# A two-block fp32 model on one core: first products from unscaled inputs, split weight queues, convolutions by pairs

## The chip, the cores and the metric

One core of a Trainium2 chip runs the whole program. The metric is device microseconds (us) of one execution. Engines are named as in the profile: PE (TensorE; PEld is its weight load), DVE (VectorE), ACT (ScalarE), POOL (GpSimd), SP (SyncE, which issues the transfers).

## The reference

The model has 512 tokens of width 1024, all in fp32: a first block (two gated feed-forward parts, a mixer of sparse attention and a state-space scan, and a gate, "ple"), and a second block of two layers. What matters here is the end of the first and the start of each layer of the second:

```python
def first_block(x, p, ...):
...
        h = h + 0.5 * swiglu(rmsnorm(h, norm_ffn2[i]), ffn2_w1[i], ffn2_w3[i], ffn2_w2[i])
        gate = jax.nn.sigmoid(rmsnorm(h, norm_ple[i]) @ w_ple_gate[i])
        h = h + gate * (p[i] @ w_ple[i])
    return rmsnorm(h, norm_final)
...
def second_block(x, c, ...):
...
    c_act = jax.nn.silu(c)
    for l in range(DEPTH_2):
        mod = c_act @ w_ada[l] + b_ada[l]
        shift, scale, gate = jnp.split(mod, 3, axis=-1)
        h = rms_norm(x, norm_g[l]) * (1.0 + scale[:, None, :]) + shift[:, None, :]
        u = h @ w_in[l]
        rg_x, rg_z, ml_x, ml_o, ml_z = jnp.split(u, split_pts, axis=-1)
        y_rg = rglru(causal_depthwise_conv(rg_x, ...), ...) * jax.nn.silu(rg_z)
        y_ml = mlstm_branch(ml_x, ml_o, ...) * jax.nn.silu(ml_z)
        y = jnp.concatenate([y_rg, y_ml], axis=-1) @ w_out[l]
        x = x + gate[:, None, :] * y
    return rms_norm(x, final_g)
```

## The kernel before, in words

**Layout.** An activation is held transposed, as 8 tiles `h[d]` of 128 channels by 512 tokens. Each fp32 product is made of three matmuls 128x512 (`mm3`, L121): high part of the weight by high part of the input, high by low, low by high. An input tile is split into `xnh` (made on ACT) and `xnl` (on DVE).

**Weights.** All weights come as 304 chunks of 8 blocks of 128x128 (512 KB) in the order of use (`Stream`, L56). SP loads a chunk into `wstage`, ACT makes its high part `whi` (L96), DVE its low part `wlo` (L98). `get` (L108) hands out a block; when it hands out the fifth block of a chunk, it queues both parts of the chunk after the next, one behind the other. Engines run their instructions in the order in which the program queues them, so a part stands in ACT's or DVE's queue at the place where `get` was called. `hold` and `release` keep back this queueing at the end of `ple` and of `out0`.

**Norms.** `Norm` adds the squares of the tiles (ACT squares, DVE and POOL add). `early` sums the first seven tiles over the channels by matmuls with a column of ones, `mean` the last one; `rsqrt` is a chain of small DVE operations and gives `ncol`; `part2` spreads it by four PE transposes to a row `nrow` (ACT copies it out of PSUM).

**The two seams.** At the start of layer 0 (`between`, L1348) and layer 1 (`renorm`, L1378) the norm is formed from the last tile of `ple` or of `out0`. Then `modulate` (L1320) makes the eight input tiles: `mt` = h by the row (DVE and POOL in turn), `xnh` on ACT, `mx` and `xnl` on DVE. The first products of a layer (`proj4`, L1490) are the four output tiles 16 to 19 (`ml_x`), which are accumulated side by side, input tile by input tile. Each is copied into a padded tile `cpad`, and a causal convolution of four taps follows on DVE for all four (`ml_in`: one `conv` with L1507, three with L1509), then the order string `LAYER` (L1385): P24 is the product of output tile 24, U24 its use, qkv0 the block-diagonal products, and so on. Layer 0 also scales x by the norm of block 1 and stores it for the residual (`residual`, L1367, as `aside`).

**Beside ffn2**, `second_prepare` forms the modulation: 48 rows of `w_ada` are loaded and reduced on DVE (`adaj`, L1219). The gate's input `p` is loaded and split there too (`split_p`, L2072).

Of the kernel before, what the change touches and what calls it, by code (L numbers as in the profile page):

```python
# [31 lines left out]
T = 512  # L32
# [3 lines left out]
CH = 8  # L36


R1, R2 = 0.27, 0.26
# [8 lines left out]
GAPS = {"base": 288, "ffn1": 320, "ffn2": 0, "lay": 320, "mix2": 224, "ple": 256}  # L48
# [7 lines left out]
class Stream:  # L56
# [4 lines left out]
    SPLIT = 2  # L61

    def __init__(self, k, dram, nchunks):
        self.k, self.dram, self.n = k, dram, nchunks
        self.order = []
        self.stage, self.hi, self.lo = {}, {}, {}
        self.loaded = self.split_done = 0
        self.pos = 0
        self.hold = False
# [14 lines left out]

    def split(self, upto):
        k = self.k
        while self.split_done < min(upto, self.n):
            c = self.split_done
            self.load(c + 1)
            st = self.stage.pop(c)  # L90
            hi = k.whi.tile([128, CH * 128], F32R, name="whi")
            lo = k.wlo.tile([128, CH * 128], F32R, name="wlo")
            n = 2 if c < 2 else 1
            for i in range(n):
                s = slice(i * CH * 128 // n, (i + 1) * CH * 128 // n)
                k.nc.scalar.activation(hi[:, s], st[:, s], AF.Copy)  # L96
                eng = k.nc.gpsimd if c * i == 1 else k.nc.vector
                eng.tensor_sub(lo[:, s], st[:, s], hi[:, s].bitcast(F32))  # L98
            self.hi[c], self.lo[c] = hi, lo
            self.split_done += 1  # L100
            self.load(c + 1 + self.AHEAD)
# [28 lines left out]
class Norm:  # L130
# [3 lines left out]
    def __init__(self, k, n, pool=None, tail=False):  # L134
        self.k, self.n, self.i = k, n, 0
        self.tail, self.head = tail, None
        self.pool = pool or k.work
        self.acc = []

    def add(self, src, scale=1.0):  # L140
# [4 lines left out]
        if own:  # L145
            sq = self.pool.tile([128, T], F32, name="nacc", bufs=3 if self.pool is k.work else 6)
# [3 lines left out]
        if own:  # L150
            self.acc.append(sq)
        elif i % 2:
            k.nc.gpsimd.tensor_add(self.acc[1], self.acc[1], sq)  # L153
        else:
            k.nc.vector.tensor_add(self.acc[0], self.acc[0], sq)
        self.i += 1
        if self.i == self.n - self.tail:
            eng = k.nc.vector if self.tail else k.nc.gpsimd
            eng.tensor_add(self.acc[0], self.acc[0], self.acc[1])
# [1016 lines left out]
def second_prepare(k, pool, ins):  # L1176
# [15 lines left out]
    for l in range(2):  # L1192
# [8 lines left out]
        L.bif = k.const2.tile([128, 8], F32, name=f"bif{l}")  # L1201
        L.v = lambda name, l=l: k.vec[:, VEC[f"{name}.{l}"][0]:VEC[f"{name}.{l}"][0] + VEC[f"{name}.{l}"][1]]
# [13 lines left out]
        def acc(i, L=L, boxes=boxes):  # L1216
# [3 lines left out]
                                   op0=OP.mult, op1=OP.add, accum_out=L.mod[:, i:i + 1])  # L1220

# [21 lines left out]
        for i in range(24):  # L1243
            step(1.4, acc, i)
            if i < 21:
                step(0.1, load, i + 3)
            if i % 12 == 7:
                step(0.3, fold, i // 12)
                if i < 12:
                    step(0.1, wload, 1)  # L1250

# [24 lines left out]
def ple(k, pool, xs, norm, pt, on_tile, early):  # L1276
# [3 lines left out]
    def gate1(m, pg):  # L1280
        ts[m] = pool.tile([128, T], F32, name="pleg", bufs=2)
# [16 lines left out]
    for m in range(8):  # L1298
# [12 lines left out]
        k.ws.hold = m == 7  # L1311
# [4 lines left out]
    early()  # L1316


def modulate(k, l, norm, gg, scr):
# [4 lines left out]
    with k.tc.tile_pool(name=f"modulate{l}", bufs=3) as tmp:  # L1324
        def scale(d):
            t = tmp.tile([128, T], F32, name="mt", bufs=4)
            if d % 2:
                nc.gpsimd.tensor_mul(t, k.h[d], norm.row)
            else:
                v.tensor_mul(t, k.h[d], norm.wide)  # L1330
            ts.append(t)
        for d in range(3):
            scale(d)
        for d in range(8):
            x = tmp.tile([128, T], F32, name="mx")
            hi, lo = xtile(k, "xnh"), xtile(k, "xnl")
            nc.scalar.activation(hi, ts[d], AF.Identity, scale=gg[:, d:d + 1], bias=L.mod[:, d:d + 1])
            v.tensor_scalar(x, ts[d], gg[:, d:d + 1], L.mod[:, d:d + 1], op0=OP.mult, op1=OP.add)
            if d + 3 < 8:
                scale(d + 3)  # L1340
            v.tensor_sub(lo, x, hi.bitcast(F32))
            xs.append((hi, lo))
            if d == 1:
                k.ws.release()
            k.dbg(f"hh{l}{d}", x)
    return xs


def between(k, scr, nf, ng):

    nc, v = k.nc, k.nc.vector
    gg = k.work.tile([128, 8], F32, name="gg")
    gf = k.vec[:, VEC["norm_final"][0]:VEC["norm_final"][0] + 8]
    v.tensor_mul(gg, gf, k.lay[0].gs)
    nf.part1(root=False)
    ng.mean()
    ms = k.work.tile([128, 4], F32, name="nmt", bufs=2)
    v.scalar_tensor_tensor(ms, nf.ms, 1e-6, ng.ms, op0=OP.mult, op1=OP.add)  # L1360
    ng.col = k.work.tile([128, 4], F32, name="ncol", bufs=2)
    rsqrt(k, ng.col, ms)
    ng.part2()
    xs = modulate(k, 0, ng, gg, scr)
    rsqrt(k, nf.col, nf.ms)

    def root():  # L1367
        nf.part2()

    def residual(d):  # L1370
        v.scalar_tensor_tensor(k.h[d], k.h[d], gf[:, d:d + 1], nf.row, op0=OP.mult, op1=OP.mult)
        nc.sync.dma_start(scr["x"][d], k.h[d])
        k.dbg(f"x2{d}", k.h[d])
    return xs, [root] + [lambda d=d: residual(d) for d in range(8)]


def renorm(k, l, norm, scr):
    norm.part1()  # L1378
    norm.part2()
    xs = modulate(k, l, norm, k.lay[l].gs, scr)  # L1380
    return xs, [lambda d=d: k.nc.sync.dma_start(scr["x"][d], k.h[d]) for d in range(8)]
# [85 lines left out]
def layer(k, l, xs, aside, ins, scr, norm, out):  # L1467
# [4 lines left out]
    with ExitStack() as st:  # L1472
        pool = st.enter_context(k.tc.tile_pool(name=f"lay{l}", bufs=1))
        room(pool, "lay")
# [15 lines left out]
        def proj4(ms):  # L1490
            pp = [bank(k) for _ in ms]
            for d in range(8):
                for ps, m in zip(pp, ms):
                    mm3(k, ps, k.ws.get((win, d, m)), xs[d], d == 0, d == 7)
            return pp
# [30 lines left out]
        G = k.ps.tile([128, T], F32, name="pm", bufs=2)  # L1526
# [698 lines left out]
```

## Time and profile before

| | |
|---|---|
| median of 3 runs (lowest, highest) | 1997.06 us (1995.61, 1997.36) |
| profiled execution: its own time; span | 1996.86 us; 1995.1 us |
| mean granted PE clock | 0.982 |
| PE busy | 1931.2 us (97%) |
| DVE, ACT, POOL busy | 1311.4 (66%), 821.4 (41%), 164.4 us (8%) |

Busy time is the time in which an engine works on an instruction. A granted clock of 1.00 is PE's level of 2.4 GHz, 0.50 its level of 1.2 GHz. In a timeline a start is followed by a duration; matmuls overlap, so the distance of two starts is the time that one takes from the next.

### The profile page before, as it was taken

The page shows a single profiled execution, that of the slowest core. Times are in us where ns is not written, and L with a number is a line of the kernel's source. Part 1 is how long each engine was busy: PE and PEld are TensorE (multiplying, and loading weights), DVE is VectorE, ACT ScalarE, POOL GpSimd, SP SyncE. Part 2 cuts the span into 40 slices and gives each one's busy share as a digit, 9 for nine tenths or more (in the row PEclk, how much of TensorE's full clock was granted, in tenths as well). Part 3 has the DMA queues.
Part 4 walks back from the last instruction along what each step waited for, and adds up shares of the span by engine and source line. Part 5 has one row for each costly group of instructions (what it writes and reads, how often), then busy time and mean ns, then how long its engine had stood idle before and what let it go on. Part 6 is the DMA issues. An engine that isn't in the chain of part 4 may idle for free. (4 is left out here: it accounts for less than half of the span.)

```text
span 1995.1 us, 24709 instructions
## 1 busy us (share of the span) xinstructions
PE 1931.2 (97%) x9320; PEld 1581.3 (79%) x9320; DVE 1311.4 (66%) x2157; ACT 821.4 (41%) x1233; POOL 164.4 (8%) x225
## 2 busy tenths in 40 slices
PE   8999999998999999999999799999999899999997
PEld 6888888887867888888878687888888677887886
DVE  7766576678655575665666675887763666877843
ACT  5323232436555432232244445555432354555521
POOL 1000000111233100000001100101000100101001
PEclk9999999998899999999999899999999899999999
DMA  5335445465301365455433143222242243222241
GB/s 184 103 116 154 158 139 159 143 194 171 103 1 33 117 218 180 158 197 190 162 104 92 55 147 118 74 75 86 88 153 87 64 156 109 70 89 86 74 155 56
DMA packets 101400, 240.10 MB, mean 120 GB/s; under 512 B 24472, under 2 KB 37528, under 8 KB 101280
## 3 DMA queue, kind: packets, MB, share of 16 engines
q1 hardware_dynamic: 100592, 237.82, 37.6%
q8 instruction: 73, 1.20, 0.2%
q10 hardware_dynamic: 688, 0.70, 0.1%
q14 instruction: 47, 0.39, 0.1%
HBM read 216.19 MB, written 21.10 MB: 119 GB/s over the span
## 5 line engine op out<-in xcount | busy, mean ns | idle before, releaser
L98 DVE TENSOR_TENSOR wlo<-wstage,whi 128x1024 fp32r<-128x1024 f32 (+1 forms) x305 | 377.3, 1245 | 147.6 <-ACT whi L96 143.8
L96 ACT ACTIVATE whi<-wstage 128x1024 fp32r<-128x1024 f32 (+1 forms) x306 | 314.0, 1045 | 139.9 <-PE pasecond L126 43.1
L276 ACT ACTIVATE t<-t 128x512 f32<-128x512 f32 x44 | 27.9, 634 | 158.5 <-DVE t L275 158.5
L127 PE MATMUL pahead<-xnh,wlo 128*128 128x512 f32 x208 | 81.3, 391 | 3.4 <-DVE wlo L98 3.4
L125 PE MATMUL pahead<-xnh,whi 128*128 128x512 f32 x208 | 83.3, 400 | 0.0
L153 POOL TENSOR_TENSOR nacc<-nacc,nsq 128x512 f32<-128x512 f32 x20 | 26.8, 1343 | 680.9 <-ACT nsq L149 680.9
L126 PE MATMUL pahead<-xnl,whi 128*128 128x512 f32 x208 | 81.1, 390 | 0.0
L125 PE MATMUL pbfirst<-xnh,whi 128*128 128x512 f32 x176 | 70.4, 400 | 7.6 <-ACT whi L96 6.5
L125 PE MATMUL pbhead<-xnh,whi 128*128 128x512 f32 x192 | 76.9, 400 | 0.0
L1509 DVE SCALAR_TENSOR_TENSOR conv<-cpad,vec,conv 128x512 f32<-128x512 f32 x96 | 72.2, 752 | 5.6
L127 PE MATMUL pbhead<-xnh,wlo 128*128 128x512 f32 x192 | 75.5, 393 | 0.0
L126 PE MATMUL pbhead<-xnl,whi 128*128 128x512 f32 x192 | 75.3, 392 | 0.0
L126 PE MATMUL pbfirst<-xnl,whi 128*128 128x512 f32 x176 | 69.5, 395 | 0.3 <-DVE xnl L222 0.3
L127 PE MATMUL pbfirst<-xnh,wlo 128*128 128x512 f32 x176 | 69.2, 393 | 0.0
L125 PE MATMUL pbsecond<-xnh,whi 128*128 128x512 f32 x176 | 68.9, 392 | 0.0
L125 PE MATMUL pafirst<-xnh,whi 128*128 128x512 f32 x176 | 68.7, 390 | 0.0
L127 PE MATMUL pafirst<-xnh,wlo 128*128 128x512 f32 x176 | 68.6, 390 | 0.0
L127 PE MATMUL pbsecond<-xnh,wlo 128*128 128x512 f32 x176 | 68.5, 389 | 0.0
L126 PE MATMUL pbsecond<-xnl,whi 128*128 128x512 f32 x176 | 68.5, 389 | 0.0
L126 PE MATMUL pafirst<-xnl,whi 128*128 128x512 f32 x176 | 68.5, 389 | 0.0
L127 PE MATMUL pasecond<-xnh,wlo 128*128 128x512 f32 x176 | 68.5, 389 | 0.0
L125 PE MATMUL pasecond<-xnh,whi 128*128 128x512 f32 x176 | 68.5, 389 | 0.0
(762 smaller groups left out, 5229.9 us busy)
## 6 DMA issues: line engine op xcount, KB each, us to landing
wstage<-in_wpack_dram SPq DMA_DIRECT2D x304, 512.0 KB, 3.7
adaw<-in_wada_dram SPq DMA_DIRECT2D x48, 512.0 KB, 4.5
scr_v<-vv SPq DMA_DIRECT2D x16, 256.0 KB, 2.2
vr<-scr_v SPq DMA_DIRECT2D x16, 256.0 KB, 4.4
xr<-scr_x SPq DMA_DIRECT2D x16, 256.0 KB, 5.8
h<-in_xT_dram SPq DMA_DIRECT2D x8, 256.0 KB, 5.8
s5vw<-scr_wq SPq DMA_DIRECT2D x64, 32.0 KB, 2.0
s5vb<-in_s5bq_dram SPq DMA_DIRECT2D x8, 256.0 KB, 2.7
```

The costliest lines, as they stand in the source:

```text
L96: k.nc.scalar.activation(hi[:, s], st[:, s], AF.Copy)
L98: eng.tensor_sub(lo[:, s], st[:, s], hi[:, s].bitcast(F32))
L125: mm(ps, w[0], x[0], start=start, stop=False)
L126: mm(ps, w[0], x[1], start=False, stop=False)
L127: mm(ps, w[1], x[0], start=False, stop=stop)
L153: k.nc.gpsimd.tensor_add(self.acc[1], self.acc[1], sq)
L276: nc.scalar.activation(t1, t1, AF.Silu)
L1509: v.scalar_tensor_tensor(c, xp[:, 1 + j:1 + j + T], w(j), c, op0=OP.mult, op1=OP.add)
```

## The change

1. **First products from raw input.** The four first output tiles of a layer are formed from x = h·g (g the norm's gain times 1 + scale), before the norm is known. These raw tiles are split as soon as each `h[d]` of `ple` or `out0` is ready (`split_raw`). The products run in the order `RAW`: input tiles 0 to 6 of each output tile first, the eighth last. The norm is formed between them (`hooks`: `early`, `mean` and `part2` after products 10, 13 and 17 in layer 0, after 1, 3 and 9 in layer 1). Afterwards each output tile is multiplied by `nrow` on DVE, and a bias `L.sw` is added on ACT (`raw_pad`). `L.sw` is the shift times these weights; it is formed beside ffn2 by 4 more transfers, 4 more DVE reductions and 8 PE transposes per layer.
2. **Input tiles of the other products** are made one operation ahead, spread over the raw products by hooks: `mt` = (h·g)·row on DVE in one operation, `xnh` on ACT, `xnl` on DVE from `mt` and the bias. POOL and `mx` are no longer used.
3. **Weight parts.** The high part is queued when the fourth block of a chunk is handed out (`HI` = 3), the low part at the seventh (`LO` = 6). `hold` and `release` are gone at the seams.
4. **Convolutions** run as two calls of two tiles.
5. **Residual.** h is stored raw in `ple` and scaled in `out0` (8 DVE operations, 4 transposes); the second one is stored in `out0`.
6. **p** is loaded and split at the start of `ple`; squares of tile 6 in `ple` are added after the last tile's gate.

```diff
     SPLIT = 2
+    HI, LO = 3, 6
...
     def get(self, *blocks):
...
-        self.split(c + 1 + (0 if self.hold else self.SPLIT if r >= CH // 2 else self.SPLIT - 1))
+        if not self.hold:
+            self.high(c + self.SPLIT + (r >= self.HI))
+        self.split(c + 1 + (0 if self.hold else self.SPLIT - 1 + (r >= self.LO)))
...
+        step(1.4, sacc, 0)
+        step(0.1, sload, 3)
+        for i in (1, 2, 3):
+            step(1.4, sacc, i)
...
+def split_raw(k, src, g, hi, lo):
+
+    k.nc.scalar.activation(hi, src, AF.Copy, scale=g)
+    k.nc.vector.scalar_tensor_tensor(lo, src, g, hi.bitcast(F32), op0=OP.mult, op1=OP.subtract)
+    return hi, lo
...
+    def scale(d):
+        t = k.ytile("mt")
+        v.scalar_tensor_tensor(t, k.h[d], gg[:, d:d + 1], norm.wide if d == 0 else norm.row, op0=OP.mult, op1=OP.mult)
+        ts.append(t)
+
+    def tile(d):
+        for e in range(d + 1 if d else 0, min(d + 2, 8)):
+            scale(e)
+        t, b = ts[d], L.mod[:, d:d + 1]
+        hi, lo = xtile(k, "xnh"), xtile(k, "xnl")
+        nc.scalar.activation(hi, t, AF.Identity, bias=b)
+        v.scalar_tensor_tensor(lo, t, b, hi.bitcast(F32), op0=OP.add, op1=OP.subtract)
+        xs.append((hi, lo))
+    return xs, tile
...
+RAW = [(m, d) for m in range(4) for d in range(7)]
+RAW = RAW[:14] + [(0, 7)] + RAW[14:21] + [(1, 7)] + RAW[21:] + [(2, 7), (3, 7)]
...
+def seam(k, l, norm, gg, early, mean, at):
+
+
+    xs, tile = modulate(k, l, norm, gg)
+    hooks = dict(zip(at, (early, mean, norm.part2)))
+    for d in range(8):
+        hooks[at[2] + 1 + d * min(14, 30 - at[2]) // 7] = lambda d=d: tile(d)
+    hooks["row"] = at[2]
+    return xs, hooks
...
+    return (*seam(k, 0, ng, gg, early, mean, (10, 13, 17)), [lambda: rsqrt(k, k.closing, nf.ms)])
...
+    return (*seam(k, l, norm, k.lay[l].gs, norm.early, norm.part1, (1, 3, 9)), [])
...
+        def raw_pad(i, ps):
+
+            xp = pool.tile([128, T + 4], F32, name="cpad", bufs=5)
+            nc.gpsimd.memset(xp[:, 0:4], 0.0)
+            v.tensor_mul(xp[:, 4:], ps, before.row)
+            nc.scalar.activation(xp[:, 4:], xp[:, 4:], AF.Identity, bias=L.sw[:, i:i + 1])
+            pads[16 + i] = xp
...
-        for m, ps in enumerate(proj4([16, 17, 18, 19])):
-            ml_pad(m, ps)
-        if l == 0:
-            aside.pop(0)()
-        ml_in(range(4))
+        banks, ready = [bank(k) for _ in range(4)], []
+        for n, (i, d) in enumerate(RAW):
+            mm3(k, banks[i], k.ws.get((win, d, 16 + i)), raw[d], d == 0, d == 7)
+            if n in hooks:
+                hooks[n]()
+            if d == 7:
+                ready.append(i)
+            while ready and n >= hooks["row"]:
+                i = ready.pop(0)
+                raw_pad(i, banks[i])
...
+        ml_in((0, 1))
+        ml_in((2, 3))
...
         for m in range(8):
+            if l == 0:
+                v.scalar_tensor_tensor(xr[m], xr[m], k.v("norm_final", m), pb, op0=OP.mult, op1=OP.mult)
...
             norm.add(k.h[m])
+            if l == 0:
+                raw.append(split_raw(k, k.h[m], k.lay[1].gs[:, m:m + 1], xtile(k, "xnh"), tile("xnl", F32R)))
+                nc.sync.dma_start(scr["x"][1, m], k.h[m])
```

**What moves on PE, at the first seam.** In these names `pbple` is the last product of `ple`, `pagates` and `pbgates` are the banks of the four first output tiles, `nacc` the sums of squares. Before:

```order
L126 MATMUL pbple<-pp1l,whi 128x512
L127 MATMUL pbple<-pp1h,wlo 128x512
L165 MATMUL pm<-ones,nacc 128x1 x16
L195 MATMUL pm<-ident,ncol 128x128 x4
L125 MATMUL pagates_9242<-xnh,whi 128x512
L126 MATMUL pagates_9242<-xnl,whi 128x512
L127 MATMUL pagates_9242<-xnh,wlo 128x512
```

And in the changed kernel, the start of the raw products, and the place of the norm's last sum and of the transposes:

```order
L146 MATMUL pbple_9169<-pp1l_8719,whi_9071 128x512
L147 MATMUL pbple_9169<-pp1h_8718,wlo_9083 128x512
L145 MATMUL pagates0_9191<-xnh_8833,whi_9071 128x512
...
L192 MATMUL pm_9264<-ones_123,nacc_9178 128x1 x4
L192 MATMUL pm_9271<-ones_123,nacc_9180 128x1 x4
...
L147 MATMUL pagates0_9193<-xnh_8933,wlo_9195 128x512
L222 MATMUL pm_9312<-ident_114,ncol_9279 128x128 x4
L145 MATMUL pagates0_9193<-xnh_8989,whi_9214 128x512
```

The sums and the transposes no longer stand between `ple` and the first product; they stand between products that do not need them.

**What moves on DVE, behind that seam.** `mt`, `mx` and `xnl` make the input tiles, `xml` is the low part of a padded tile, `wlo` a weight's low part. Before, the input tiles come first, right behind `ncol`:

```order
L213 SCALAR_TENSOR_TENSOR ncol<-rsa,rsy 128x4
L1330 TENSOR_TENSOR mt<-h,pm 128x512 x2
L1338 TENSOR_SCALAR mx<-mt,gg,mod_5923 128x512
L1341 TENSOR_TENSOR xnl<-mx,xnh 128x512
L1338 TENSOR_SCALAR mx<-mt,gg,mod_5923 128x512
L1330 TENSOR_TENSOR mt<-h,pm 128x512
L1341 TENSOR_TENSOR xnl<-mx,xnh 128x512
L98 TENSOR_TENSOR wlo<-wstage,whi 128x1024
```

Now, at the last two of the eight input tiles and behind them:

```order
L1389 SCALAR_TENSOR_TENSOR mt_9409<-h_108,gg_8722,nrow_9317 128x512
L1398 SCALAR_TENSOR_TENSOR xnl_9412<-mt_9395,mod0_5920,xnh_9411 128x512
L1555 TENSOR_TENSOR cpad_9418<-pagates0_9193,nrow_9317 128x512
L1398 SCALAR_TENSOR_TENSOR xnl_9426<-mt_9409,mod0_5920,xnh_9425 128x512
L1555 TENSOR_TENSOR cpad_9429<-pbgates0_9194,nrow_9317 128x512
L1569 TENSOR_SCALAR conv_9436<-cpad_9319,vec_92 128x512
L1571 SCALAR_TENSOR_TENSOR conv_9436<-cpad_9319,vec_92,conv_9436 128x512 x3
L1607 TENSOR_TENSOR xml_9441<-cpad_9319,xmh_9434 128x512
L108 TENSOR_TENSOR wlo_9444<-wstage_9304,whi_9404 128x1024
```

The four scalings into `cpad` now lie among the input tiles, and one convolution stands ahead of the low part `wlo_9444`, which the third input tile of the second product behind the seam (P25) reads.

**What moves on SP.** The loads of p stood among ffn2's weights; now they come behind all of them, with gate weights behind them:

```order
L82 DMA wstage_8702<-in_wpack_dram 128x1024
L2156 DMA p0_8710<-in_pT_dram 128x512
L2156 DMA p1_8712<-in_pT_dram 128x512
L82 DMA wstage_8754<-in_wpack_dram 128x1024
L82 DMA wstage_8819<-in_wpack_dram 128x1024
L2180 DMA scr_x_88<-h_90 128x512
```

Two chunks of the gate's weights, and every later one, are queued behind p on SP.

## Rows read from the trace of the kernel before

**Rows 1.** The page: busy shares, and PE's granted clock in 40 slices.
```profile
PE 1931.2 (97%) x9320; PEld 1581.3 (79%) x9320; DVE 1311.4 (66%) x2157; ACT 821.4 (41%) x1233; POOL 164.4 (8%) x225
...
PEclk9999999998899999999999899999999899999999
```

**Rows 2.** Windows: length; busy PE, PEld, DVE, ACT, POOL; PEclk; DMA share; GB/s.
```profile
720.00:1015.00 295.00, 293.65 (x1323) 242.91 (x1322) 184.66 (x266) 80.01 (x95) 0.00 (x0) 1.00 0.54 178
1118.40:1134.40 16.00, 6.86 (x37) 6.13 (x36) 8.53 (x26) 4.17 (x8) 1.50 (x2) 0.67 0.07 27
1134.40:1141.00 6.60, 5.26 (x12) 3.78 (x13) 6.39 (x8) 4.71 (x6) 2.29 (x2) 0.50 0.00 0
1165.00:1450.00 285.00, 282.37 (x1440) 233.00 (x1439) 214.14 (x343) 153.36 (x221) 21.32 (x32) 0.99 0.31 96
463.90:467.00 3.10, 3.03 (x7) 2.11 (x8) 2.68 (x4) 0.35 (x1) 0.00 (x0) 0.50 0.93 280
```

**Rows 3.** Timeline of PE, first seam: start, duration, work, [idle before, releaser].
```profile
1118.17 0.39 PE L127 MATMUL pbple<-pp1h,wlo 128*128 128x512 f32 x1
1120.33 1.02 PE L165 MATMUL pm<-ones,nacc 128*128 128x1 f32 x8 [1.78 <-DVE nacc L159]
...
1125.02 3.57 PE L165 MATMUL pm<-ones,nacc 128*128 128x1 f32 x16 [2.26 <-ACT nacc L149]
1131.10 1.09 PE L195 MATMUL pm<-ident,ncol 128*128 128x128 f32 x4 [2.52 <-DVE ncol L213]
1134.45 0.79 PE L125 MATMUL pagates<-xnh,whi 128*128 128x512 f32 x1 [2.26 <-ACT xnh L1337]
...
1160.38 0.39 PE L125 MATMUL pbgates<-xnh,whi 128*128 128x512 f32 x1
...
1161.06 0.60 PE L195 MATMUL pm<-ident,ncol 128*128 128x128 f32 x4
1161.42 0.48 PE L125 MATMUL pagates<-xnh,whi 128*128 128x512 f32 x1
```

**Rows 4.** Timeline of PE, second seam.
```profile
1554.36 0.39 PE L127 MATMUL pbout<-ymh,wlo 128*128 128x512 f32 x1
...
1590.19 0.39 PE L125 MATMUL pagates<-xnh,whi 128*128 128x512 f32 x1
```

**Rows 5.** Timeline of DVE behind the first seam, and the release of the row.
```profile
1132.86 0.69 DVE L1330 TENSOR_TENSOR mt<-h,pm 128x512 f32<-128x512 f32 x1 [1.90 <-ACT nrow L198]
...
1167.00 0.69 DVE L1586 SCALAR_TENSOR_TENSOR xcs<-xcs,conv 128x512 f32<-128x512 f32 x1
1167.60 1.22 DVE L98 TENSOR_TENSOR wlo<-wstage,whi 128x1024 fp32r<-128x1024 f32 x1
1168.73 0.54 DVE L1507 TENSOR_SCALAR conv<-cpad,vec 128x512 f32<-128x512 f32 x1
1169.38 2.33 DVE L1509 SCALAR_TENSOR_TENSOR conv<-cpad,vec,conv 128x512 f32<-128x512 f32 x3
1171.62 0.69 DVE L1546 TENSOR_TENSOR xml<-cpad,xmh 128x512 fp32r<-128x512 f32 x1
1172.23 0.69 DVE L1586 SCALAR_TENSOR_TENSOR xcs<-xcs,conv 128x512 f32<-128x512 f32 x1
```

**Rows 6.** Lines of tile mx, 1100 to 1200: count, shortest/median/longest ns.
```profile
L1338 DVE TENSOR_SCALAR mx<-mt,gg,mod x8: 533/541/1627, 1134.1 to 1147.5; 128x512 f32<-128x512 f32 x8
```

**Rows 7.** Waits of PE in the whole span: total, times, longest.
```profile
PE pahead L127 <- DVE wlo L98: 3.4, 2, 1.7
PE pasecond L125 <- ACT gh L233: 3.1, 2, 2.3
```

**Rows 8.** Timeline of DVE beside ffn2, at the split of p.
```profile
1030.85 0.69 DVE L234 TENSOR_TENSOR pp0l<-p,pp0h 128x512 fp32r<-128x512 f32 x1 [3.76 <-ACT pp0h L233]
```

**Rows 9.** Lines of tile adaj: the reductions beside ffn2.
```profile
L1219 DVE CUSTOM_DVE_ANT_0 adaj<-adaw,b2c,vec x48: 1274/1278/1282, 710.2 to 1013.7; 128x1024 f32<-128x1024 f32 x48
```

**Rows 10.** Waits of DVE in the whole span.
```profile
DVE wlo L98 <- ACT whi L96: 143.8, 131, 6.4
```

**Rows 11.** Timeline of PE in the mixer, at its longest wait.
```profile
463.97 0.76 PE L125 MATMUL pbmix<-xnh,whi 128*128 128x512 f32 x1 [4.83 <-DVE ropeo L612]
```

More of the change, by code (lines that the diff above doesn't have):

```diff
@@ L36 @@
 CH = 8
[L39 removed]
+R1, R2 = 0.27, 0.30
 class Ctx:
     pass
[L48 removed]
+GAPS = {"base": 288, "ffn1": 320, "ffn2": 160, "lay": 384, "mix2": 224, "ple": 256}
 def room(pool, name):
@@ L145, in add @@
         if own:
-            sq = self.pool.tile([128, T], F32, name="nacc", bufs=3 if self.pool is k.work else 6)
+            sq = self.new("nacc")
         else:
@@ L1273, in second_prepare, with ple @@
     return steps
-def ple(k, pool, xs, norm, pt, on_tile, early):
+def ple(k, xs, norm, pt, on_tile):
     nc, v = k.nc, k.nc.vector
@@ L1323, in modulate @@
     xs, ts = [], []
[L1324 to L1374, printed above, removed]
@@ new lines, in modulate, with between, early, mean @@
+    return xs, tile
[8 more added lines that the diff above has]
+    return xs, hooks
+def between(k, nf, ng, gg):
+    v = k.nc.vector
+    def early():
+        nf.early()
+        ng.early(0.0)
+    def mean():
+        nf.mean()
+        ng.mean()
+        ms = k.work.tile([128, 4], F32, name="nmt", bufs=2)
+        v.scalar_tensor_tensor(ms, nf.ms, 1e-6, ng.ms, op0=OP.mult, op1=OP.add)
+        ng.col = k.work.tile([128, 4], F32, name="ncol", bufs=2)
+        rsqrt(k, ng.col, ms)
+    return (*seam(k, 0, ng, gg, early, mean, (10, 13, 17)), [lambda: rsqrt(k, k.closing, nf.ms)])
@@ L1464, in ending, with layer @@
     last(1, 6, False, nc.sync)
-def layer(k, l, xs, aside, ins, scr, norm, out):
+def layer(k, l, raw, xs, hooks, aside, before, ins, scr, norm, out):
     nc, v = k.nc, k.nc.vector
@@ L2088, in body @@
-        norm = None
+            swiglu(k, st["xs"], st["norm"], "ffn2_w1", "ffn2_w3", "ffn2_w2", (6, 6, 5, 5),
+                   lambda d: feed("norm_ple", d), R2, ((0, 1, 5), (1, 0, 7)), "ffn2")
+            k.fill.drain()
+        k.phase = "ple"
+        k.lpool = pool("lay")
+        room(k.lpool, "lay")
+        k.ytile = lambda name, dtype=F32: k.lpool.tile([128, T], dtype, name=name, tag="y", bufs=k.NX)
+        pt = []
+        for d in range(2):
+            t = k.ytile(f"p{d}")
+            nc.sync.dma_start(t, ins["pT"][d * 128:(d + 1) * 128])
+            pt.append(t)
@@ new lines, in body, with done @@
+        later = []
+        def done(m):
+            if m == 6:
+                raw.append(split_raw(k, k.h[m], gg[:, m:m + 1], k.ytile("xnh", F32R), k.ytile("xnl", F32R)))
+            nf.add(k.h[m], 1.0, later if m == 6 else None)
+            ng.add(k.h[m], k.v("norm_final", m), later if m == 6 else None)
+            for f in later if m == 7 else ():
+                f()
+            if m != 6:
+                raw.append(split_raw(k, k.h[m], gg[:, m:m + 1], k.ytile("xnh", F32R), k.ytile("xnl", F32R)))
+            nc.sync.dma_start(scr["x"][0, m], k.h[m])
@@ L2089, in body @@
+        ple(k, st["xs"], st["norm"], pt, done)
+        before = ng
+        xs, hooks, aside = between(k, nf, ng, gg)
         for l in range(2):
@@ L2091, in body @@
             k.phase = f"layer{l}"
-            layer(k, l, xs, aside, ins, scr, norm, out)
+            raw = layer(k, l, raw, xs, hooks, aside, before, ins, scr, norm, out)
             if l == 0:
-                xs, aside = renorm(k, 1, norm, scr)
+                before = norm
+                xs, hooks, aside = renorm(k, 1, norm)
         return k.ws
```

172 lines of the change are left out of this document (96 added, 76 removed).

## The prediction, made before the changed kernel ran

> **What bounds the kernel now.** I read the page first: PE is busy 97% of the span, DVE 66%, ACT 41% [rows 1]. So a microsecond is won only where PE stands still or runs at its lower clock. The PEclk line shows where that is: four slices of 40 at 8, and little else. The windows say how much. In the long stretches PE works without a break: 293.65 us of 295 beside ffn2, 282.37 of 285 in the heads of layer 0 [rows 2]. At the first seam it is busy 6.86 us of 16, and the next 6.6 us run at a granted clock of 0.50, the 1.2 GHz level [rows 2].
>
> The timeline of PE then shows the chain. After the last gate matmul at 1118.17 PE waits for the sums of squares (1.78 and 2.26), for `ncol` (2.52) and for the first input tile (2.26), and the first product starts only at 1134.45 [rows 3]. Three matmuls of one product take 1161.06 - 1160.38 = 0.68 us, that is 0.227 per matmul [rows 3]. The last gate matmul so ends its turn at 1118.39. The 32 products of the four first output tiles and four transposes are through at 1161.42: 43.0 us for 32 x 0.68 = 21.8 us of work at full clock. At the second seam the same stretch runs from 1554.59 to 1590.19, 35.6 us [rows 4]. All of the gain must come from these two places; elsewhere PE hardly waits.
>
> **The change part by part**, with T = 0 at the end of the last matmul ahead of a seam.
>
> *First seam, PE.* The raw products follow the last gate matmul at once: the first reads the chunk of weights that matmul read, and a raw tile that was split long before. What PE has to do until P24 is 21.8 us of products, four column sums of 8 matmuls, and four transposes. A group of 8 sums lasts 1.02 us, less a tail of 0.39 - 0.23 for the overlap, so 0.9; the transposes take 1161.42 - 1161.06 = 0.36 [rows 3]. That is 21.8 + 3.6 + 0.4 = 25.8. One low part now stands on DVE behind the last gate tile and its sums, and I put 0.6 of stall on it: P24 starts at T = 26.4 in place of 43.0, a gain of **16.6**. The norm itself is hidden: `ncol` took 2.5 us from the sum's end to the transposes [rows 3], and four products, 2.7 us, now stand between them.
>
> *Second seam, PE.* 21.8 + 2 x 0.9 + 0.4 = 24.0 in place of 35.6: 11.6. The early sum (0.9) stood inside `out0` and no longer does, the residual's four transposes (0.4) are new there: **12.1**.
>
> *DVE behind the seams: what comes late next.* The work between the row and the first convolutions is no less than before, and PE arrives 16 us earlier. From the transposes to DVE's first use of the row took 1131.10 to 1132.86, 1.8 us [rows 3, 5]. The transposes stand behind 18 products and the sums: T = 12.3 + 3.6 + 0.6 = 16.5, the row is usable at 18.3. DVE then has 8 `mt`, 8 `xnl` and 3 `cpad` ahead of the last `xnl`, 0.6 each by the distance of two such operations (1167.00 to 1167.60), and one `wlo` of 1.13 (1167.60 to 1168.73) [rows 5]: 11.4 + 1.1, so T = 30.8 if it never waits. P24 needs that tile at 26.4 + 7 x 0.68 = 31.2. But each `xnl` waits for its `xnh`, and ACT has `whi` and the bias of `cpad` in between; walking both queues I get 33.5: a stall of 2.3. Then come `cpad` (0.6), a convolution with its `xml` (1168.73 to 1172.23, 3.5) and the `wlo` (1.13) that P25 reads at its third tile: T = 38.7, needed at 26.4 + 2.3 + 10 x 0.68 + 0.4 = 35.9, a stall of 2.8 to 3.2. The next chunk's low part comes 6.4 us later (convolution and `xml` 3.5, two `xcs` 1.2, `xcl` 0.6, `wlo` 1.1), where PE needs 8 x 0.68 = 5.4 for a chunk: 1.1. The one after keeps up, and a last one costs 1.6. In all **-8.2**. The low end is DVE without any wait on ACT (30.8): 2.7 + 1 = 3.7; the high end is 12, with the 0.8 us more of each half of the `xnl` pairs. I take the walk, as the order of both queues is known.
>
> At the second seam the hooks sit at 1, 3 and 9 and the tiles from 10 on, some six products earlier; by the same walk 0.1 + 1.6 = **-1.7** is left (0 to 4).
>
> What an input tile costs on DVE: `mx` took 541 ns in the median, and 1627 at the longest, where POOL's `mt` ran beside it [rows 6]. It is replaced by an operation of two tensors (0.6 us to the next), and POOL's half of `mt` comes to DVE. The Trainium skill ("VectorE: DVE Perf Modes", The perf-mode tier table) has `tensor_scalar` in fp32 at twice the rate of operations on two tensors. By that rule alone the change makes DVE slower by about 1 us a seam; by the row the long cases, which go with POOL's part, are worth as much, so I set the difference at nothing.
>
> *p at the gate's start.* Beside ffn2 the split of p made DVE wait 3.76 for ACT [rows 8], and behind it PE waited 2.3 once on the split gate tile [rows 7]. That goes: **+2.6** with the small wait for the low part that followed. At its new place p's transfer waits for the end of ffn2 and two ACT and two DVE operations stand ahead of the gate's norm; PE has products of the gate to do there, so between 0 and -1.5, I take **-0.5**, as the row's use is some products away. The gate weights that are queued on SP behind it are loaded over two chunks ahead, 11 us.
>
> *Shift.* Sixteen transposes on PE at 0.36 for four: **-1.4**. Eight reductions of 1.278 us [rows 9] are 10.2 us on DVE, which is busy 184.66 of 295 us there [rows 2], and eight transfers at a DMA share of 0.54: nothing, unless DVE's queue holds up a `wlo`.
>
> *Raw splits and residual.* 8 splits in `ple`, 8 splits and 8 scalings in `out0`, some 15 us on DVE in 157 us that are not full: nothing.
>
> *Weight parts.* `whi` is queued one block earlier, `wlo` two blocks (1.37 us) later. DVE stood 143.8 us waiting for `whi` in 131 places [rows 10]; these waits mostly go, so DVE's queue runs ahead. In the heads PE waited twice 1.7 us for a `wlo` [rows 7]. Of this 3.4 I take **+1** (0 to 3.4), since the later place eats some of it.
>
> *Clock.* An idle time of 4.83 us [rows 11] was followed by 3.1 us at 0.50 [rows 2], 1.55 us lost. The stalls forecast above are shorter, up to 3.2; I take **-1** (0 to -3). The Trainium skill ("TensorE: Matmul & The Clock Gate", Part 1) says that the throttled state is the default and activity lifts it; the rows agree with both levels.
>
> **Sum:** 16.6 + 12.1 - 8.2 - 1.7 + 2.6 - 0.5 - 1.4 + 1 - 1 = 19.5. The profiled execution took 1996.86 us, which is the median of the runs shown within 0.2, so the forecast is **1977.4**. Two tenths of a per cent, 4 us, is about what a measurement of this kernel can tell from no change.
>
> **The rivals.**
>
> *The seams close.* DVE runs ahead, since the waits on `whi` are gone, and neither seam stalls: only 1.5 of the 9.9 us of stalls remain, no clock is lost and the heads' waits go. For it: DVE alone would be in time for P24 (30.8 against 31.2). Against it: the convolution ahead of the `wlo` is 3.5 us at a place where PE leaves 0. Sum 19.5 + 8.4 + 1 + 1.4: about **1967**.
>
> *DVE becomes the bound behind both seams.* Stalls of 12 and 4 us, and each drops the clock as after the idle time above (3 us in all): 28.7 - 16 - 3 + 2.6 - 1.5 - 1.4 = 9.4, about **1987.5**. For it: DVE's order puts all four scalings and a convolution ahead of weights; against it: the second seam's hooks are early.
>
> *Low parts come late everywhere.* `wlo` is queued 1.37 us later on each of some 300 chunks. Where DVE is behind, PE then waits at the third matmul of a chunk's first block. In the heads DVE is busy 214.14 of 285 us [rows 2], so a low part may stand behind long runs of convolution and scan. From 20 / 1.37, about 15 chunks, that wait by the full delay, the gain is gone; 45 such chunks cost 62 us: 1977 + 62 = 2039, and 25 of them about **2011**. Against it: PE waited there twice in the whole span [rows 7], and the waits on `whi` that go are larger than the delay.
>
> *The overlap is there but not the gain*: the norm's sums wait inside the raw products, so PE stands at `early` or the transposes for as long as before. The sums are ready when the last gate tile is squared, 1.78 + 2.26 us of waits before [rows 3]; the order puts ten products (6.8 us) ahead. It would give no change, about 1995; I see little for it.
>
> **How the numbers follow.** Forecast 0.56, closed seams 0.14, DVE as the bound 0.21, late low parts 0.05, no gain 0.04. The forecast's own case spans 1973 to 1982 by the ends of its terms, the first two rivals add 1966 to 1973 and 1982 to 1989. The range 1966 to 1989 leaves out the last two cases and a little of the first ones' ends. Faster by over 0.2%: 0.56 + 0.14 + 0.21 = 0.91; within 0.2% 0.04; slower 0.05.
>
> **What would show it.** PE's timeline should have the first `pagates` 0.23 us behind the last `pbple` and the last `pbout`, with granted clock 1.00 from 1118 to 1141. P24 should start about 26 and 24 us behind them. The waits should list `xnh` or `xnl` of the seventh and eighth input tile and `wlo` ahead of P25, some 8 us behind the first seam and 2 behind the second. The wait of `pasecond` on `gh` should be gone, and DVE's 143.8 us on `whi` largely too. The forecast is wrong if `wlo` stands among PE's waits in the heads with more than 5 us, or if the sums wait inside the raw products.

## The result and the profile after

The changed kernel takes 2015.41 us in the median of 4 runs (2015.37 to 2015.53), the kernel before 1997.21 beside it (1995.61 to 1998.67): a ratio of 1.0091, with an interval of 1.0074 to 1.0109. It is 18 us slower, where 19.5 us faster was forecast. Its profiled execution has a span of 2013.8 us. One execution of the hybrid kernel below took 6870.74 us and stands in no time or ratio given here.

The page, the same lines as [rows 1]:

```profile
PE 1941.6 (96%) x9336; PEld 1586.8 (79%) x9336; DVE 1333.4 (66%) x2189; ACT 831.9 (41%) x1252; POOL 160.8 (8%) x217
...
PEclk9999999998999999999999999999999999989999
```

The shares have hardly moved, and the dips of the clock at the seams are smaller. The time must be looked for stage by stage. In this table a stage runs from the start of its first matmul in PE's timeline to that of the next stage (a seam from the end of the last `ple` or `out0` matmul to the first product of the heads):

| stage | before, us | after, us | gain | forecast gain |
|---|---|---|---|---|
| start to ffn2 | 687.7 | 687.7 | 0 | 0 |
| ffn2 | 373.7 | 371.3 | 2.4 | 1.2 (p 2.6, shift -1.4) |
| ple | 57.1 | 58.2 | -1.1 | -0.5 |
| first seam to heads | 156.5 | 157.4 | -0.9 | 8.4, less 1 for the clock |
| heads of layer 0 | 191.7 | 202.7 | -11.0 | 0.5 |
| out0 | 88.0 | 88.1 | -0.1 | 0.5 |
| second seam to heads | 148.5 | 142.4 | 6.1 | 9.9 |
| heads of layer 1 | 190.5 | 202.5 | -12.0 | 0.5 |
| out1 and end | 101.5 | 103.6 | -2.1 | 0 |

Of the 38 us between the forecast and these gains the heads make 24, the first seam 8 and the second 4. Two things went wrong: the heads lost 23 us, and the first seam gave nothing. PE's waits in the whole span (total, times, longest) name both places:

```profile
PE pbhead L147 <- DVE wlo L108: 16.0, 6, 6.2
PE pbgates L147 <- DVE wlo L108: 7.5, 2, 4.5
...
PE pagates L145 <- ACT ml_w_q L1665: 4.7, 2, 2.5
...
PE pahead L147 <- DVE wlo L108: 3.4, 2, 1.7
...
PE paout L147 <- DVE wlo L108: 1.8, 2, 1.2
```

A low part `wlo` ends most of them; the two 1.7 us waits of [rows 7] are still there.

**The first seam.** PE's timeline after the change, and below it the windows (columns as in [rows 2]):

```profile
1116.90 0.39 PE L147 MATMUL pbple<-pp1h,wlo 128*128 128x512 f32 x1
1117.13 0.40 PE L145 MATMUL pagates<-xnh,whi 128*128 128x512 f32 x1
...
1129.24 0.50 PE L147 MATMUL pbgates<-xnh,wlo 128*128 128x512 f32 x1 [4.50 <-DVE wlo L108]
1129.58 2.94 PE L192 MATMUL pm<-ones,nacc 128*128 128x1 f32 x16
...
1151.16 0.39 PE L145 MATMUL pagates<-xnh,whi 128*128 128x512 f32 x1
...
1157.87 0.50 PE L145 MATMUL pagates<-xnh,whi 128*128 128x512 f32 x1 [1.24 <-ACT xnh L1397]
...
1164.25 0.79 PE L147 MATMUL pbgates<-xnh,wlo 128*128 128x512 f32 x1 [3.02 <-DVE wlo L108]
...
1182.36 0.50 PE L145 MATMUL pagates<-xch,whi 128*128 128x512 f32 x1 [2.16 <-ACT ml_w_q L1665]
```

```profile
1117.30:1124.60 7.30, 7.30 (x32) 5.50 (x31) 5.19 (x8) 3.33 (x5) 0.00 (x0) 1.00 0.09 36
1124.60:1129.20 4.60, 0.14 (x1) 0.00 (x0) 4.39 (x7) 3.43 (x5) 0.00 (x0) 1.00 0.53 171
1129.20:1143.00 13.80, 13.76 (x65) 12.04 (x66) 5.28 (x18) 1.02 (x2) 0.00 (x0) 0.75 0.23 78
...
1164.00:1172.00 8.00, 7.75 (x27) 6.29 (x28) 7.61 (x13) 4.38 (x9) 0.10 (x1) 0.79 0.26 70
```

The first raw product does follow the last gate matmul by 0.23 us, where it came 16.3 us behind it before [rows 3]. But in the eleventh product PE stops for 4.50 us. DVE is busy 4.39 of these 4.60 us: four additions of squares, the split of the last raw tile and then the low part itself. After the stop the granted clock is 0.75 in the mean of 13.8 us. P24 starts at 1151.16, that is T = 34.0 behind the end of the last gate matmul at 1117.13. Behind it come the forecast waits for the eighth input tile and for the second product's low part and, later, one that was not forecast, for a bank that ACT has not emptied.

DVE's first use of the row, and the last low part of an input tile that it makes:

```profile
1142.43 0.69 DVE L1555 TENSOR_TENSOR cpad<-pagates,nrow 128x512 f32<-128x512 f32 x1 [0.44 <-ACT nrow L225]
...
1157.85 0.75 DVE L1398 SCALAR_TENSOR_TENSOR xnl<-mt,mod,xnh 128x512 fp32r<-128x512 f32 x1 [1.40 <-ACT xnh L1397]
```

How late DVE is shows at the end of the fourth convolution, its last `xcl` (the low part of what the convolution gives). Before and after:

```profile
1179.86 1.48 DVE L1546 TENSOR_TENSOR xcl<-xcs,xch 128x512 fp32r<-128x512 f32 x2
```

```profile
1182.59 0.69 DVE L1607 TENSOR_TENSOR xcl<-xcs,xch 128x512 fp32r<-128x512 f32 x1
```

That is 1181.34 - 1118.39 = 63.0 us behind the end of the gate before, and 1183.28 - 1117.13 = 66.1 after. PE's work was moved; the end of DVE's came 3.1 us later.

**The second seam** has no stop in the raw products:

```profile
1565.32 0.39 PE L145 MATMUL pagates<-xnh,whi 128*128 128x512 f32 x1
...
1589.38 0.39 PE L145 MATMUL pagates<-xnh,whi 128*128 128x512 f32 x1
...
1613.95 0.50 PE L145 MATMUL pagates<-xch,whi 128*128 128x512 f32 x1 [2.51 <-ACT ml_w_q L1665]
```

P24 starts at T = 24.06; 24.0 was forecast. Here DVE did come earlier. Its last `xcl`, before and after:

```profile
1608.16 1.48 DVE L1546 TENSOR_TENSOR xcl<-xcs,xch 128x512 fp32r<-128x512 f32 x2
```

```profile
1614.19 0.68 DVE L1607 TENSOR_TENSOR xcl<-xcs,xch 128x512 fp32r<-128x512 f32 x1
```

It ends 1609.64 - 1554.59 = 55.1 us behind the end of `out0` before, and 1614.87 - 1565.32 = 49.6 after: 5.5 us earlier, in a stage that is 6.1 us shorter.

**The heads.** DVE's timeline in the first heads before the change, then the same place after it:

```profile
1322.07 1.23 DVE L98 TENSOR_TENSOR wlo<-wstage,whi 128x1024 fp32r<-128x1024 f32 x1 [2.83 <-ACT whi L96]
1323.21 0.68 DVE L1854 TENSOR_TENSOR rth<-rth,conv 128x512 f32<-128x512 f32 x1
...
1333.95 1.23 DVE L1874 TENSOR_TENSOR_SCAN ry<-ra,rth 128x512 f32<-128x512 f32 x1
1335.09 1.20 DVE L98 TENSOR_TENSOR wlo<-wstage,whi 128x1024 fp32r<-128x1024 f32 x1
```

```profile
1321.73 0.69 DVE L1915 TENSOR_TENSOR rth<-rth,conv 128x512 f32<-128x512 f32 x1 [2.83 <-ACT rth L1907]
...
1333.56 1.23 DVE L1935 TENSOR_TENSOR_SCAN ry<-ra,rth 128x512 f32<-128x512 f32 x1
1334.70 1.20 DVE L108 TENSOR_TENSOR wlo<-wstage,whi 128x1024 fp32r<-128x1024 f32 x1
```

```profile
1335.95 0.80 PE L147 MATMUL pbhead<-xnh,wlo 128*128 128x512 f32 x1 [6.20 <-DVE wlo L108]
```

Before, one low part stood ahead of the chain of the gated scan (`rth`, `ra`, `ry`). After, its place in the program is two blocks later, and that is behind the chain: it starts at 1334.70 in place of 1322.07. DVE goes into it from `ry` without idle time, so it waits neither for a transfer nor for its `whi`. PE waits 6.20 us for it, and the clock falls:

```profile
1336.00:1342.00 6.00, 6.00 (x15) 4.75 (x16) 1.63 (x2) 0.00 (x0) 0.00 (x0) 0.52 0.61 178
```

DVE's waits for `whi` did shrink as forecast, from the 143.8 us of [rows 10] to

```profile
DVE wlo L108 <- ACT whi L98: 65.0, 65, 5.5
```

but these were waits that PE did not feel.

### The profile page after: what moved, and what is told of

It reads as the page before. It is cut to its first block, busy times and chain, and to the rows that moved or that the text cites. A ratio compares the mean times of both kernels' runs of the same rounds, so it can differ in the third digit from the quotient of the medians.

```text
span 2013.8 us, 24738 instructions
## 1 busy us (share of the span) xinstructions
PE 1941.6 (96%) x9336; PEld 1586.8 (79%) x9336; DVE 1333.4 (66%) x2189; ACT 831.9 (41%) x1252; POOL 160.8 (8%) x217
## 4 chain that ended last, share of the span: by engine, by line
PE 49%; DVE 13%; ACT 5%; issue 2%; POOL 0%; DVEq 0%; ACTq 0%
PE pasecond L146 3%; PE pbsecond L147 3%; PE pbsecond L145 3%; PE pbsecond L146 3%; PE pasecond L147 3%; PE pasecond L145 3%; DVE wlo L108 2%; PE pbhead L147 2%; PE paout L147 2%; PE paout L145 1%; PE pbhead L145 1%; PE paout L146 1%; PE pbhead L146 1%; PE pahead L147 1%; PE pbgates L145 1%
## 5 line engine op out<-in xcount | busy, mean ns | idle before, releaser
L108 DVE TENSOR_TENSOR wlo<-wstage,whi 128x1024 fp32r<-128x1024 f32 (+1 forms) x305 | 382.7, 1261 | 65.1 <-ACT whi L98 65.0
```

The source lines that it names most:

```text
L108: eng.tensor_sub(self.lo[c][:, s], self.stage[c][:, s], self.hi[c][:, s].bitcast(F32))
```

## The experiments

Theory A was that a low part's later place costs the run of DVE work between the two places, not the 1.37 us between two blocks. For the first seam it was that DVE's work behind the seam is the bound. All ratios are against runs of the kernel before on the same chip.

**Place of the low part.**

```diff
-    HI, LO = 3, 6
+    HI, LO = 3, 4
```

> The changed kernel with the low part of a weight chunk queued at the fifth block (as before the change), the high part still at the fourth. Theory A (a low part that is queued two blocks later falls behind the whole run of DVE work that the order string puts between the two places, so that PE stops for up to 6.2 us at a time and its clock falls): the two head stages, 202.6 and 202.5 us in the changed kernel, go back to about 192, and the 4.5 us stop in the raw products shrinks; about 1992 us. Rival B (the heads are slower because of the transfers or of ACT, whose queue now has the high parts earlier; the place of the low part is only where it shows): the heads stay above 200, about 2013 us.

Measured 1999.23 us (1995.40 to 2002.66), ratio 1.0003 (0.9990 to 1.0016). The heads took 191.8 and 193.1 us, and `pbhead` is gone from PE's waits, as is the 4.5 us stop in the raw products; the last stage is back at 101.5 us. The total is 7 us above the 1992 expected: `ple` grew to 60.7 and the second seam to 145.7, the wait at the block-diagonal products doubled, and in `ple` PE waits for gate tiles (`pleg`), which it does not in the changed kernel:

```profile
PE pagates L145 <- ACT ml_w_q L1665: 9.2, 2, 5.0
PE pbple L145 <- DVE pleg L1339: 1.8, 3, 1.0
```

The first seam took 161.6 us; this shows nothing of the place, since the hybrid below took 161.5 there with the seventh block.

So theory A holds in the heads. In `ple` and the second seam the seventh block is the better place. PE's waits for `pleg` agree with a low part that stands behind work on gate tiles there, which is wanted sooner; no run tests this by itself.

```diff
-    HI, LO = 3, 6
+    HI, LO = 3, 3
```

> The changed kernel with both parts queued at the fourth block. Theory A: as early as possible is as good as the fifth block or a little better, 1990 to 1993 us. Rival B: no better than the changed kernel, about 2013. A third possibility C: a low part queued so early stands in front of work that PE waits for sooner (DVE waits for ACT's high part with the rest behind it, as in the kernel before, 143.8 us of such waits): 1995 to 2000.

Measured 2001.13 us, ratio 1.0013 (1.0004 to 1.0023); heads 191.8 and 191.5 us. The heads agree with A, the total lies 1 us above C's range: `ple` took 60.8 us and the second seam 146.8, the first seam 156.2. The stages ahead of ffn2 took 692.5 us in this profile, 687.7 in the changed kernel's.

**The queueing alone, in the kernel before** (its `Stream` replaced by the new one, nothing else):

> The kernel before with the new queueing of weight parts alone (high at the fourth block, low at the seventh; hold and release at the seams stay). Theory A: the loss of the heads appears here as well, two times 11 us, with the stop of 6.2 us at the same place: about 2019 us. Rival B: no such stop without the rest of the change, within 3 us of 1997.

Measured 2020.75 us, ratio 1.0112 (1.0097 to 1.0127): 22.8 us slower. The heads took 202.8 and 202.1 us, with the same stop:

```profile
PE pbhead L147 <- DVE wlo L108: 16.0, 6, 6.2
```

```profile
1332.98 0.79 PE L147 MATMUL pbhead<-xnh,wlo 128*128 128x512 f32 x1 [6.19 <-DVE wlo L108]
```

Together with the run with the fifth block this shows the cause of the loss: taken away it goes, put in alone it comes. That run left the high part at the fourth block, so it is the low part's place. The loads are queued with the low part and moved with it in both runs; that the stop is not theirs is read from DVE's timeline in the heads.

**Convolutions in one call.**

```diff
-        ml_in((0, 1))
-        ml_in((2, 3))
+        ml_in(range(4))
```

> The changed kernel with the first four convolutions in one call instead of two pairs. If the pairs help as meant (weight parts come between the pairs), the stretch from the end of the gate to the first head, 157.4 us, gets longer by 2 to 6 us at each seam: about 2022. If the pairs cost nothing and bring nothing, 2015. If the pairs are what makes the low part of the second product late, the 3.0 us stop ahead of it goes: about 2010.

Measured 2016.09 us, ratio 1.0087 (1.0072 to 1.0102), beside 1.0091 for the changed kernel; seams 159.8 and 142.6 us. The waits change their place (6.3 us for low parts in `pagates`, none at `ml_w_q`), but the pairs cost nothing and bring nothing that can be measured.

**A hybrid**: the low part at the fifth block from the first head of a layer to the end of its out products, at the seventh elsewhere.

```diff
-        self.split(c + 1 + (0 if self.hold else self.SPLIT - 1 + (r >= self.LO)))
+        late = 4 if self.k.phase[:4] == "head" or self.k.phase[:3] == "out" else self.LO
+        self.split(c + 1 + (0 if self.hold else self.SPLIT - 1 + (r >= late)))
```

> The changed kernel with the low part queued at the seventh block everywhere except from the first head of a layer to the end of its out products, where it is queued at the fifth. Theory A (what a later place costs depends on what stands between the two places: long runs of scan work in the heads, next to nothing elsewhere): heads 192 and 193 us as in the run with the fifth block, everything else as in the changed kernel, 2015 - 22 = 1993 us. Rival B (the later place is no better anywhere, the differences ahead of the heads are noise): as with the fifth block everywhere, 1999.

Measured 1989.13 us in the median of five (1988.62 to 1993.89), ratio 0.9961 (0.9945 to 0.9978). The same kernel again:

> The hybrid a second time, for a profile that belongs to its times. Heads 192 and 193 us, the stretch from the gate's end to the first head 157, the second one 142: 1990 us.

1991.59 us (1988.82 to 1997.53), ratio 0.9969 (0.9957 to 0.9982); heads 191.8 and 193.3 us, second seam 142.1. With the low parts mended, the rest of the change is worth 6 to 8 us. The first seam took 161.5 us in this profile, 4 more than in the changed kernel, though both have the same program there. Its windows show why:

```profile
1125.40:1130.10 4.70, 0.23 (x2) 0.00 (x0) 4.49 (x8) 3.39 (x5) 0.00 (x0) 0.85 0.53 167
1130.10:1144.00 13.90, 13.90 (x49) 12.36 (x50) 3.80 (x17) 0.47 (x1) 0.00 (x0) 0.50 0.23 75
```

After the same stop (4.47 us) the clock stays at 0.50 for 13.9 us, where it was 0.75 in the mean before. DVE's first use of the row (T = 29.5, against 25.3) and P24 (38.2, against 34.0) both came 4 us later, and the stage took 4.1 us longer.

**Sums two products earlier** at the first seam, in the hybrid.

```diff
-    return (*seam(k, 0, ng, gg, early, mean, (10, 13, 17)), ...
+    return (*seam(k, 0, ng, gg, early, mean, (10, 11, 15)), ...
```

> The hybrid with the norm's last sum and transposes two products earlier in the first seam (hooks 10, 11, 15 in place of 10, 13, 17). Theory A (behind the seam DVE is the bound from the moment the row is there until the fourth convolution is done, so a row that comes earlier moves everything behind it): the stretch from the gate's end to the first head is 1.4 to 2.5 us shorter than in the hybrid, about 1991. Rival B (PE then waits for the sums or the row instead): no gain, 1993 or a microsecond more.

Measured 1992.80 us, ratio 0.9979 (0.9968 to 0.9990), first seam 157.1 us: no gain. `ncol`, the norm as a column, was done 23.2 us behind the gate's end, against 23.7 in the changed kernel, since the sums still stand behind the 4.5 us stop.

**Less DVE work behind the seams**: three of four taps of the first four convolutions of each layer left out, in the hybrid and in the kernel before.

```diff
...
-            for j in (2, 1, 0):
+            for j in () if skip else (2, 1, 0):
...
```

> The hybrid with three of the four taps of the first four convolutions of each layer left out, which takes 4 x 2.25 = 9 us of DVE work from behind each seam. Theory A (DVE's work behind the seam is the bound there): the stops ahead of the second product's low part (3.2 us) and at the block-diagonal products (2.3 and 2.7) go, the first seam gets 4 to 8 us shorter and the second 2 to 4: about 1984. Rival B (the stretch is long because the norm's chain and PE's lower clock make it so): within 2 us of the hybrid.

> The kernel before with the same three taps of the first four convolutions left out. Theory A: there DVE stood idle ahead of the convolutions (2.0 us for the padded tile, 2.6 for a high part) and PE waited for none of it: within 1 us of 1997. Rival B (the convolutions bound PE already before the change): 4 us or more faster, 1993 or less.

The hybrid takes 1982.30 us, ratio 0.9919 (0.9889 to 0.9950); first seam 152.2 us, second 137.5, so 5.2 and 4.9 less than in the changed kernel. The wait at `ml_w_q` is gone, and what is left of the two at `pbgates` is the stop and 1.2 us:

```profile
PE pbgates L148 <- DVE wlo L108: 5.7, 2, 4.5
```

The complete kernels with the seventh block there and the pairs in their usual order, four profiles, took 157.1 to 161.5 us at the first seam and 140.8 to 142.4 at the second, so both gains stand clear of that spread. The hybrid's heads without taps took 195.3 and 195.0 us in this profile, at a clock of 0.97, and have no wait that the hybrid's own (191.8 and 193.3) do not have.

The kernel before does not move: 1999.10 us, ratio 0.9998 (0.9985 to 1.0011), seams 156.4 and 147.2. So the change made DVE's work behind the seams a bound that it was not before. Of the 9 us of DVE work about 5 come back on PE, at each seam.

**The low part in the raw products ahead of the last gate tile**, and the first seam's hooks at 16, 17 and 21.

```diff
     proj(7)
+    k.ws.split(k.ws.pos // CH + 3)
     gate2(7, pps[7])
...
-    return (*seam(k, 0, ng, gg, early, mean, (10, 13, 17)), ...
+    return (*seam(k, 0, ng, gg, early, mean, (16, 17, 21)), ...
```

> The hybrid with the low part of the third chunk of raw products queued ahead of the last gate tile, and the first seam's sums and transposes later (hooks 16, 17, 21 in place of 10, 13, 17), when the last squares are added. Theory A (the 4.5 us stop in the raw products comes from one low part behind the last gate tile on DVE, and the lower clock of the following 7 us comes from that stop): no stop and a granted clock of 1.00 through the raw products, the row 4 to 6 us earlier, first seam 5 to 8 us shorter than the hybrid's 157: about 1983. Rival B (DVE is the bound there as well, so the stop only moves to the sums or to the second product's low part): less than 2 us.

Measured 1989.04 us (1982.31 to 1996.35), ratio 0.9948 (0.9922 to 0.9975), which the hybrid's interval overlaps. The stop is gone; the first seam still took 158.2 us. PE and the windows:

```profile
1131.83 1.84 PE L193 MATMUL pm<-ones,nacc 128*128 128x1 f32 x16
1134.31 2.28 PE L193 MATMUL pm<-ones,nacc 128*128 128x1 f32 x16
1141.72 0.92 PE L223 MATMUL pm<-ident,ncol 128*128 128x128 f32 x4
```

```profile
1129.80:1136.00 6.20, 6.13 (x41) 5.64 (x42) 2.78 (x6) 1.41 (x2) 0.00 (x0) 0.96 0.52 171
1136.00:1143.00 7.00, 7.00 (x22) 5.64 (x23) 1.95 (x12) 0.33 (x1) 0.00 (x0) 0.55 0.01 2
```

The clock fell all the same, now behind a wait of 1.06 us and 32 one-column matmuls of the sums, with PE busy from there on. So theory A is right that the stop is from that low part, and wrong that the lower clock needs such a stop. P24 started at T = 31.0, 3 us earlier than in the changed kernel, but the row came no earlier: DVE had its first `mt` at 25.6 us, against 25.9. DVE's timeline shows why:

```profile
1138.80 0.16 DVE L241 SCALAR_TENSOR_TENSOR ncol<-rsa,rsy 128x4 f32<-128x4 f32 x1
1143.31 0.69 DVE L1557 TENSOR_TENSOR cpad<-pagates,nrow 128x512 f32<-128x512 f32 x1 [4.34 <-ACT nrow L226]
```

`ncol` was done at T = 20.7, 3 us earlier than in the changed kernel (23.7), and then waited: the transposes now stand four products later, and PE went through these at the lower clock. That P24 came earlier and the stage gained nothing agrees with DVE's work from the row on as the bound. But the run took the stop away and moved the hooks at once, so what an earlier row would be worth remains open.

**The second pair of convolutions three steps later.**

```diff
         ml_in((0, 1))
+        todo.extend([lambda: None] * 3)
         ml_in((2, 3))
```

> The hybrid with the second pair of convolutions three steps later in the queue of steps, so that ACT's copies of the first block-diagonal products stand ahead of that pair's work. Theory A (the wait of 2.2 and 2.5 us for `ml_w_q` is ACT standing in order behind the second pair, whose convolutions DVE has not done): both waits go, 2 to 5 us in all, about 1986. Rival B (a bound on DVE's sum of work: the wait comes back at the second pair's own use in the next block-diagonal products): 1990.

Measured 1986.35 us (1986.11 to 1987.32), ratio 0.9942 (0.9927 to 0.9958). The wait moves from `ml_w_q` to the next copies and shrinks from 4.7 to 3.3 us:

```profile
PE pagates L1679 <- ACT ml_w_k L1666: 3.3, 2, 1.7
```

The second seam takes 139.9 us in place of 142.1, and 139.9 again in the next run; the run before this one took 140.8 without the edit, so not all of the difference need be the edit's. The median is the lowest of the complete kernels, 11 us below the one before and 29 below the change; its interval overlaps the hybrid's.

> The hybrid with the early low part and the late second pair together. If the two stops are independent their gains add: about 1979 to 1981. If both are only DVE's sum of work behind the seam, no better than the better of the two.

Measured 1990.29 us (1981.79 to 1992.84), ratio 0.9955 (0.9937 to 0.9974): no gain on the better of the two shows in the total. In its profile the seams are the shortest of all complete kernels with raw products, 155.8 and 139.9 us; what is lost stands in the heads of layer 0, where neither edit is. They took 195.3 us at a clock of 0.97, with the same waits as the hybrid's 191.8 us at 0.99:

```profile
1273.10:1468.40 195.30, 192.65 (x968) 161.32 (x966) 151.72 (x259) 98.28 (x136) 16.63 (x22) 0.97 0.26 79
```

```profile
1279.50:1471.30 191.80, 189.26 (x967) 158.76 (x966) 151.39 (x259) 98.14 (x136) 17.08 (x22) 0.99 0.27 81
```

So whether the gains add is open; the times of this kernel spread over 11 us.

## Why the prediction was wrong

- **Weight parts: the step that failed.** I priced a low part queued two blocks later at 1.37 us, two blocks of PE's time, and set the waits in the heads at +1. The third rival had the mechanism, with the same price per chunk and a chance of 0.05; that its 25 chunks at 1.37 us gave 2011, close to the result, is luck, as six waits in the heads made the loss. Measured: three new waits a layer, 8.0 us together with one of 6.2, and a clock of 0.52 behind that one; 23 us in both layers, and with them the 2.1 us of the last stage, which is back at 101.5 us with the fifth block. What counts is what the order puts between the two places on DVE, here 13 us of the scan's chain (1321.73 to 1334.70), 2.8 of them DVE's own waits for ACT. The order of the changed kernel was there to be read: I read it at the seams and not in the heads, where I went by an average of busy time, 214 of 285 us. The waits for `whi`, my argument against that rival, were not PE's.
- **First seam, PE: a term mis-sized.** 0.6 us of stall for one low part was 4.5: I did not add up DVE's queue ahead of it. With the clock behind it (13.8 us at 0.75, 3.4 us lost) these are 7.3 of the 7.6 us by which P24 starts late, 34.0 against 26.4. I had allowed 1 us for the clock in all. The clock's part is not shown to be the stop's: the run with the early low part lost as much (7.0 us at 0.55) without it. I had also read the clock's price too low. Behind the idle time of [rows 11] I took 3.1 us at 0.50; the next window of that trace adds 0.75 us, 2.3 lost in all:

```profile
467.00:472.00 5.00, 5.00 (x22) 4.05 (x20) 3.92 (x6) 2.83 (x5) 1.81 (x2) 0.85 0.37 70
```

- **First seam, DVE behind it: close, in part by luck.** Stalls of 8.2 us were forecast; measured are 7.0: 1.24 + 0.29 + 0.25 for input tiles (2.3 forecast), 3.02 for P25's low part (up to 3.2) and 2.16 at the block-diagonal products, where I had 1.1 and 1.6 at low parts. With 1.7 us of lower clock (8 us at 0.79 from 1164) that is 8.7 of the 9.9 us by which the rest of the stage grew. DVE first used the row at T = 25.3, not 18.3, which is most of the 7.6 again. From there to the end of the last `xnl` it took 16.2 us, where the walk gave 15.2. The runs without taps show that this work became the bound; the second rival had that, with 12 and 4 us of stall where 7.0 and 2.7 were measured behind P24.
- **Second seam: right at P24, short behind it.** 24.06 against 24.0. Of the stalls I had 1.7; measured are 2.51 at `ml_w_q` and 0.2 at a low part, and 1.7 us go to a lower clock behind them (4.4 us at 0.61 from 1614). The kernel before, too, was misread by one product: there P24 started at 1589.51, T = 34.9 and not 35.6, so 0.7 us of the forecast gain was never there:

```profile
1589.28 0.39 PE L127 MATMUL pbgates<-xnh,wlo 128*128 128x512 f32 x1
1589.51 0.39 PE L125 MATMUL pagates<-xnh,whi 128*128 128x512 f32 x1
```

- **p and the shift: right in sign.** ffn2 gained 2.4 us (1.2 forecast), `ple` lost 1.1 (0.5). The change also raises the pace at which the steps beside ffn2 are handed out (`R2` from 0.26 to 0.30), and no run separates the three.
- **DVE's price of an input tile** was set at nothing, and no run shows what the old tiles would have cost at the new place. The 1.0 us by which DVE took longer than the walk is about what the sixteen operations `mt` and `xnl` took more than it gave them, 0.66 us from one start to the next (1145.24 to 1145.90) in place of 0.6. No run here separates the Trainium skill's rule on `tensor_scalar` ("VectorE: DVE Perf Modes", The perf-mode tier table) from POOL's part in the 1627 ns of [rows 6]. At 512 columns [rows 5] show 0.54 us for a `tensor_scalar` and 0.69 for an operation on two tensors, less than that rule's factor of two.
- **A sum of the first rival** is off by 1 us: of the heads' 3.4 us of waits the forecast had taken 1, so 2.4 and not 1.4 were left, about 1966.

## What to carry to other kernels

When an instruction is queued later in an engine's order, its price is not the time between the two calls on the engine that asks, but the work, with its waits, that stands between the two places in the queue it goes to. Read that queue at every place where it is long and serial, not as a mean of busy time. And where products are moved under a chain to hide it, ask which engine does the chain and what follows: if its own finish does not come earlier, the waits only move behind the products. At the first seam DVE's finish came 3.1 us later and the stage gained nothing; at the second it came 5.5 us earlier and the stage gained 6.1.

## What was not expected of the hardware

After the same stop of 4.5 us the granted clock came back at different times: a mean of 0.75 in the next 13.8 us in one execution, 0.50 through 13.9 us in another. The same stage took 157.4 and 161.5 us. In the heads of layer 0 the same waits, the longest of 1.7 us, went with a clock of 0.99 in one execution and 0.97 in two others, and the stage took 191.8 and 195.3 us. So a change of a few microseconds can't be read from one profile. And the clock fell to 0.55 without a stop longer than 1.06 us, behind 32 matmuls of one column each, with PE busy; what made it fall there was not tested.
